# Sums of h finished ahead of the K/V block, key copies in fewer transfers, first compressed probabilities turned inside the attention slots

## The chip, the core and the metric

The kernel runs on one core of one Trainium2 chip. The metric is the device time of one execution in microseconds (us), lower is better. TensorE is called PE here (PEld its weight loads), VectorE DVE, ScalarE ACT, GpSimd POOL, SyncE SP. POOL and SP also issue the transfers (DMA).

## What is computed

One layer of a decoder trunk for 512 tokens of 2048 channels, all in float32. Of the reference, cut to what matters here:

```python
h = rms_norm(x, norm_g)
q, kv, g_logits, z_a, uv, z_b, merge_logits = split(h @ w_in)
k_c, v_c, k_s, v_s, k_w, v_w = split(kv, 6)        # 4 groups x 64 each
kc, vc = compress(k_c, ...), compress(v_c, ...)    # 32 -> 1 token, stride 16
# per head: softmax over compressed, selected and window keys, ALiBi slopes
o = g0 * softmax(q kc) vc + g1 * softmax(q k_s) v_s + g2 * softmax(q k_w) v_w
o_a = o * silu(z_a)
o_b = spatial_gating(uv) * silu(z_b)
merged = g_a * (o_a @ w_up_a) + g_b * (o_b @ w_up_b)
x = x + merged @ w_out
x = x + sigmoid(x @ w_ple_gate) * (p @ w_ple)
out = rms_norm(x, final_g)
```

## The kernel before

**Precision.** PE multiplies in a rounded float32 format, so each operand is split into a high part (a cast on ACT, `high`, line 158) and a low part (source minus high on DVE, `low`, line 164), and each product is three matmuls: high by high, high by low, low by high (lines 420 to 422, 446 to 448 and 459 to 461). The weights are streamed by SP into `raw` (three buffers) and split into `hi` and `lo`, or `hs` and `ls` in the blocks; `split_to` does it two steps ahead of the matmuls. `hi` has four buffers and `lo` three.

**One stream of matmuls.** All projections are jobs of one generator, `gemm`. `fill(n)` draws n units from it (a unit is three matmuls of 512 columns, about), `finish(name)` runs it to the end of a job. Between units the program places other work by hand. Three small queues hang on it: `deferred` (done at the next step's `flush`), `background` (taken at `state["pops"]` entries for each step) and `slow` (transfers that add up weights in DRAM for later blocks, taken at `state["rate"]` for each step; each is led by a one-column copy on ACT and POOL, `pad_r`, lines 378 and 379). Job order at the start: p by its weights (pl0 to pl3), kc0, vcg (compressed values and gate logits), kc1, q0, q1, kv, za0, q2, and so on.

**The K/V block** (`kv`) computes the selected and window keys and values, 1024 columns, with seven products in place of eight on 2x2 halves: products "1" to "7", four steps each, 12 matmuls of 512 columns a step (lines 420 to 422). The steps go in the order of `products(job)`: 1 and 5 in turn, 6 and 3 in turn, 7, then 2 and 4 in turn. Products 5, 6, 3 and 7 need sums of parts of h in place of h. The sums of weights are DVE subtractions (line 301).

**The sums of h** are made by `h_chunk(c)`, four chunks of four background entries: `whole`, `s1`, `s23`, `s4`. A chunk is eight additions or subtractions of 128x512 on DVE (line 504, into the scratch `o32`) and four splits (ACT cast, DVE low): into `ob_h` (sum 5), `ob_l` (sum 6), `vt` (sum 3) and into a pair of stream buffers of `hi` and `lo` (sum 7, tiles `h_hi` and `h_lo`). Each is then stored to DRAM by POOL (`hsum` line 528, `h3_d` line 535) for later blocks, and sum 7 is read back into `ob_h` before product 7 (line 828). The background begins with four splits of the compression weights `w1` (into `w1h` and a `b11` buffer).

**Keys.** When rows of keys are done, `turn_k(b, hf)` turns them on PE (`ps_kt`, line 592) and splits them into `ob_h` and `ob_l` (lines 597 and 603); b is 0 or 1 for the two branches. Each half (hf) is then copied to the other 64 partitions with four transfers by POOL (line 608), 16 in all.

**Between the block and the attention slots** six single units with flushes follow, then the first group's compressed attention is started: `cmp_scores` (two matmuls, line 1463, with `kcp`, that POOL clears at line 1325 and fills at line 1454), `cmp_softmax`, `cmp_weigh` (POOL multiplications, lines 1504 and 1505), `cmp_transpose` (line 1511), with 1, 3, 3, 5 and 1 units between. Then 48 slots of the attention follow (`slots`; a slot is a head pair ft, a block of 128 queries and one or both branches), with the units of the remaining q and za jobs spread over them. For groups 1 to 3, softmax, weighing and turning stand in the slots j = 1, 2 and 4 of ft = 2, 4, 6.

Some names share a tag in the profile: `o` is `o32`, `b` is a `b11` buffer (a q head pair after line 160 and 166), `c` is `c21`, `keep` the kept partial results of a block, `t` the DRAM sums of w_up_b.

Of the kernel before, what the change touches and what calls it, by code (L numbers as in the profile page):

```python
# [13 lines left out]
F32 = mybir.dt.float32  # L14
# [46 lines left out]
def products(job):  # L61

    if isinstance(job.order[0], tuple):
# [7 lines left out]
                             ("6", "0123"), ("7", "3"), ("5", "0123"), ("4", "1"), ("3", "0123")) for j in map(int, js)]  # L71
LATE_BANK = {"1": 0, "7": 0, "6": 1, "5": 1, "3": 1, "2": 2, "4": 3}


@with_exitstack
def kernel(ctx: ExitStack, tc: tile.TileContext, x, p, norm_g, w_in,
# [121 lines left out]
    def add_job(job):  # L198
        jobs.append(job)
        if job.kind == "S":  # L200
# [10 lines left out]
            if job.reload:  # L211
                for tags in (("b11", "b12"), ("b22",), ("b11'",), ("b21",)):
                    for j in range(half // 2):
                        for tag in tags:
                            c, k = (job.c0, c2)[tag[2] == "2"], half * (tag[1] == "2") + 2 * j
                            ld[tag, j] = add_load("b12" if tag == "b12" else "raw", weights(job, k, 2, c), 2, job.cols)
                for p, j in products(job):
                    for tag in {"5": ("b11",), "3": ("b22",), "7": ("b11'",), "4": ("b21", "b12")}.get(p, ()):
                        last_sub[ld[tag, j]] = len(subs)
                    subs.append((job, p, j, ld))  # L220
                return
# [287 lines left out]
    def parts_later(hi, lo, src, then=None):  # L509
# [9 lines left out]
        deferred.append(first)  # L519

    def h_chunk(c, temps, homes):

# [3 lines left out]
        def put(p, src):  # L526
            o = homes[p][:, k1]
            parts_later(o[:, :, lo_t], o[:, :, hi_t], src, lambda: nc.gpsimd.dma_start(hsum_dram[p][:, k1], o))

# [58 lines left out]
    def turn_k(b, hf):  # L588
# [10 lines left out]
        def lows():  # L599
            for a in range(2):  # L600
                for e in range(2):
                    g = kk(b, 2 * a + e)
                    nc.vector.tensor_tensor(out=ob_l[rows[e], g, sl], in0=ps[rows[e], a * 256:a * 256 + 256],
                                            in1=ob_h[rows[e], g, sl].bitcast(F32), op=ALU.subtract)
            for o in (ob_h, ob_l):
                for e in range(2):
                    g = slice(kk(b, e), 8, 4)
                    nc.gpsimd.dma_start(o[rows[1 - e], g, sl], o[rows[e], g, sl])
        deferred.append(lows)

    vc_rows = {}
# [210 lines left out]
    def evac_kv(p, ps):  # L822
# [3 lines left out]
        if p == "5":  # L826
            for c in range(4):
# [4 lines left out]
    add_job(Job("kv", "S", w_in, C_KV + 1024, 512, KT, lambda p, k, t: kv_act(p, k, t), evac_kv, ("s", "g", "t"),  # L832
                c2=C_KV + 512, reload=True))
    for s in "z0 q2 q3 z1 q4 q5 z2 q6 q7 z3 z4 z5 z6 z7".split():
# [368 lines left out]
    with tc.tile_pool(name="cmp", bufs=1) as cmp:  # L1203
# [24 lines left out]
        for c in range(4):  # L1228
            background.extend(h_chunk(c, lambda: [o32[:, i].rearrange("p (a t) -> p a t", a=2) for i in range(4)],
                                      {"5": ob_h, "6": ob_l, "3": vt_flat}))  # L1230
        state["pops"] = 0.75
        finish("kc0")
        state["pops"] = 0.4
        finish("vcg")
        state["pops"] = 0.75
        fill(4)
# [71 lines left out]
    assert not background  # L1308
    for _ in range(6):
        fill(1)  # L1310
        flush()
# [13 lines left out]
    nc.gpsimd.memset(kcp.bitcast(F32), 0.0)  # L1325
    nc.gpsimd.memset(vcb.bitcast(F32).rearrange("p i e -> p (i e)"), 0.0)
    b0 = att.tile([P, S], F32, name="b0")
# [192 lines left out]
    def cmp_values(ft):  # L1520
        b = bank("s", "ps_c")
        for n, i in enumerate((0, 1 + ft % 2)):
# [9 lines left out]
                            base=384, channel_multiplier=1)  # L1532
    cmp_scores(0, 0)
    for f, u in zip((partial(cmp_scores, a=1), cmp_softmax, cmp_weigh, cmp_transpose), (1, 3, 3, 5)):
        fill(u)
        flush()
        f(0)
    fill(1)
    n = len(slots)
# [6 lines left out]
    for s in range(n + 3):  # L1546
# [21 lines left out]
        if s < n:  # L1568
            if ft % 2 == 1 and ft < 7 and j == 3:
                events.append((cmp_keys, (ft + 1) // 2))  # L1570
            if ft % 2 == 0 and ft > 0 and j in (1, 2, 4):
                events.append(({1: cmp_softmax, 2: cmp_weigh, 4: cmp_transpose}[j], ft // 2))
            if ft % 2 and j == 3:
                events.append((cmp_values, ft))
# [612 lines left out]
```

## Time and profile before

| what | us |
|---|---|
| median of 3 runs | 1530.21 (1528.96 to 1530.72) |
| the profiled execution, device time | 1529.65 |
| its span, first to last instruction | 1527.9 |
| mean granted PE clock in it | 0.995 of full speed |

Times in the lines of the profile are us from the span's start; outside the span lie 1.75 us. A line of a group or of the timeline reads: line, engine, operation, out<-in, shape, count, and in brackets the idle time of the engine just before and what ended it. A table of windows gives an engine's busy time in each stretch (number of instructions in brackets), the granted PE clock, and how busy the 16 DMA engines were.

### The profile page before, as it was taken

How to read it: one execution, taken by the hardware profiler on the slowest of the kernel's cores; microseconds unless marked ns; L12 is line 12 of the kernel's file. 1: busy time of each engine (PE TensorE's matmuls, PEld its weight loads, DVE VectorE, ACT ScalarE, POOL GpSimd, SP SyncE). 2: the span in 40 equal slices, each digit the busy share in tenths (PEclk: the TensorE clock that was granted, in tenths of full speed). 3: DMA queues.
4: the chain of work that ended last, by engine and by line, in shares of the span. 5: the costliest groups of instructions: out<-in, count | busy, mean ns of one | idle time of the engine just before them, and what ended most of it. 6: DMA issues, size and time to landing. Idle time of an engine off the chain costs nothing.

```text
span 1527.9 us, 20459 instructions
## 1 busy us (share of the span) xinstructions
PE 1500.1 (98%) x7149; PEld 1252.8 (82%) x7149; DVE 1245.7 (82%) x1889; ACT 868.7 (57%) x1498; POOL 396.3 (26%) x617
## 2 busy tenths in 40 slices
PE   9998979999999999999999999999999999999997
PEld 8986868888888888888888888888888888888886
DVE  7598768998997788978897979797877985678877
ACT  6545446777775555545555565555446465544556
POOL 1222062334343232343334333431010002100000
PEclk9999999999999999999999999999999999999999
DMA  8577698889884985878586977896697769945555
GB/s 324 159 226 231 190 198 213 184 176 237 183 222 141 307 274 164 272 184 271 141 260 179 253 204 233 246 333 251 236 333 253 237 198 322 316 171 179 184 204 191
DMA packets 184855, 346.82 MB, mean 227 GB/s; under 512 B 15144, under 2 KB 77232, under 8 KB 181552
## 3 DMA queue, kind: packets, MB, share of 16 engines
q0 software_dynamic: 71696, 172.62, 41.4%
q1 hardware_dynamic: 112912, 172.64, 34.6%
q8 instruction: 56, 0.92, 0.2%
q14 instruction: 47, 0.39, 0.1%
q10 hardware_dynamic: 144, 0.26, 0.0%
HBM read 283.08 MB, written 109.58 MB: 257 GB/s over the span
## 4 chain that ended last, share of the span: by engine, by line
PE 90%; DVE 5%; issue 2%; ACT 1%; POOL 1%; DVEq 0%; POOLq 0%; ACTq 0%
PE ps_m L420 7%; PE ps_m L422 7%; PE ps_m L421 7%; PE ps_wo L421 3%; PE ps_wo L420 3%; PE ps_wo L422 3%; PE ps_t L1409 2%; PE ps_u L420 2%; PE ps_u L422 2%; PE ps_ub L421 2%; PE ps_ub L420 2%; PE ps_pg L422 2%; PE ps_pg L421 2%; PE ps_ua L421 2%; PE ps_ua L420 2%
## 5 line engine op out<-in xcount | busy, mean ns | idle before, releaser
L164 DVE TENSOR_TENSOR ls<-b,hs 128x1024 fp32r<-128x1024 f32 x224 | 273.7, 1222 | 112.2 <-ACT hs L158 110.8
L158 ACT CAST hs<-b 128x1024 fp32r<-128x1024 f32 x224 | 235.6, 1053 | 206.0 <-PE ps_m L422 47.5
L158 ACT CAST hs<-raw 128x1024 fp32r<-128x1024 f32 x130 | 136.9, 1054 | 126.7 <-issue 35.7
L164 DVE TENSOR_TENSOR ls<-raw,hs 128x1024 fp32r<-128x1024 f32 x130 | 158.7, 1221 | 40.1 <-ACT hs L158 39.8
L420 PE MATMUL ps_m<-hs,act_h 128*128 128x512 f32 x256 | 100.1, 391 | 0.0
L421 PE MATMUL ps_m<-ls,act_h 128*128 128x512 f32 x256 | 99.7, 389 | 0.0
L422 PE MATMUL ps_m<-hs,act_l 128*128 128x512 f32 x256 | 99.6, 389 | 0.0
L301 DVE TENSOR_TENSOR b<-raw,b 128x1024 f32<-128x1024 f32 x76 | 92.6, 1218 | 4.7 <-DMA raw<-in_w_in_dram 4.6
L164 DVE TENSOR_TENSOR lo<-raw,hi 128x512 fp32r<-128x512 f32 (+1 forms) x120 | 79.4, 666 | 19.7 <-issue 6.6
L158 ACT CAST hi<-raw 128x512 fp32r<-128x512 f32 (+1 forms) x120 | 70.4, 597 | 38.2 <-PE ps_vcg L461 11.5
L301 DVE TENSOR_TENSOR b<-b,b 128x1024 f32<-128x1024 f32 x72 | 87.6, 1217 | 0.0
L379 POOL COPY pad_r<-pad_r 128x1 f32<-128x1 f32 x40 | 34.9, 872 | 159.2 <-ACT pad_r L378 159.2
L158 ACT CAST pth<-ps_t 128x512 fp32r<-128x512 f32 (+1 forms) x88 | 47.7, 544 | 46.8 <-PE ps_t L1409 46.2
L1368 ACT ACTIVATE prob<-prob,st 128x512 f32<-128x512 f32 (+3 forms) x128 | 70.7, 556 | 4.8 <-DVE st L1359 4.7
L164 DVE TENSOR_TENSOR ptl<-ps_t,pth 128x512 fp32r<-128x512 f32 (+1 forms) x88 | 55.5, 636 | 11.8 <-ACT pth L158 11.1
L1359 DVE CUSTOM_DVE_ANT_0 prob<-ps_s,b 128x512 f32<-128x512 f32 (+3 forms) x128 | 56.1, 485 | 1.6 <-PE ps_s L1350 1.1
L422 PEld LDWEIGHTS ps_m<-hs,act_l 128*128 128x128 f32 x256 | 48.1, 188 | 10.1
L421 PEld LDWEIGHTS ps_m<-ls,act_h 128*128 128x128 f32 x256 | 48.1, 188 | 9.9
L420 PEld LDWEIGHTS ps_m<-hs,act_h 128*128 128x128 f32 x256 | 48.1, 188 | 9.8
L446 PE MATMUL ps_za<-act_h,hi 128*128 128x512 f32 x128 | 54.5, 426 | 0.0
L1384 DVE TENSOR_SCALAR prob<-prob,st,gates 128x512 f32<-128x512 f32 (+3 forms) x128 | 51.5, 454 | 1.8
L446 PE MATMUL ps_q<-act_h,hi 128*128 128x512 f32 x128 | 52.3, 409 | 0.0
(746 smaller groups left out, 4556.9 us busy)
## 6 DMA issues: line engine op xcount, KB each, us to landing
raw<-in_w_in_dram SPq DMA_DIRECT2D x112, 512.0 KB, 5.1
b<-in_w_in_dram SPq DMA_DIRECT2D x58, 512.0 KB, 6.6
o<-in_w_out_dram POOLq DMA_DIRECT2D x48, 512.0 KB, 7.9
t<-in_w_up_b_dram POOLq DMA_DIRECT2D x24, 512.0 KB, 8.5
raw<-in_w_ple_gate_dram SPq DMA_DIRECT2D x24, 512.0 KB, 3.8
b<-o SPq DMA_DIRECT2D x18, 512.0 KB, 6.5
o<-o POOLq DMA_DIRECT2D x16, 512.0 KB, 5.1
act_l<-gate POOLq DMA_DIRECT2D x8, 1024.0 KB, 13.2
```

Of the source, the lines that this page charges most:

```text
L158: nc.scalar.copy(hi, src)
L164: nc.vector.tensor_tensor(out=lo, in0=src, in1=hi.bitcast(F32), op=ALU.subtract)
L301: nc.vector.tensor_tensor(out=b[o], in0=b[x], in1=b[y], op=ALU.subtract)
L379: nc.gpsimd.tensor_copy(steps[:, 16 + i:17 + i], steps[:, i:i + 1])
L420: nc.tensor.matmul(o, ah, wh, start=st, stop=False, skip_group_check=go)
L421: nc.tensor.matmul(o, ah, wl, start=False, stop=False, skip_group_check=go)
L422: nc.tensor.matmul(o, al, wh, start=False, stop=sp, skip_group_check=go)
L446: nc.tensor.matmul(ps, hi[:, j], ah, start=st, stop=False)
L1359: nc.vector.tensor_tensor_reduce(out=pt[:, j * n:j * n + n], in0=o[:, j], in1=b0[:, 512 - n:], scale=-SLOPE[h], scalar=3.0e38, op0=ALU.add ...
L1368: nc.scalar.activation(sl, sl, AF.Exp, bias=st[:, 0, j, hh:hh + 1], scale=-1.0, accum_out=st[:, 1, j, hh:hh + 1])
L1384: nc.vector.tensor_scalar(out=sl, in0=sl, scalar1=st[:, 1, j, hh:hh + 1], scalar2=gates[:, i, gate:gate + 1], op0=ALU.mult, op1=ALU.mult)
L1409: nc.tensor.transpose(b[:, (2 * e + hh) * P:(2 * e + hh + 1) * P], pts[hh][:, c:c + P], ident)
```

## The change

- `h_chunk`: only the store of sum 5 is issued as soon as the sum is made. The stores of sums 6 and 3 are collected and put into the background behind the last chunk; there the rate falls to one entry for two steps. Ahead of it the rates are higher: 1, 0.8 and 0.7 entries a step (0.75, 0.4 and 0.75 before).
- The loads of the K/V block: the first b11 and b12, then b12 ahead of b11.
- The block's last steps go 2, 2, 4, 2, 4, 2, 4, 4 in place of 2, 4, 2, 4, 2, 4, 2, 4.
- Keys: the copies to the other partitions move both halves at once, four transfers for each b. Those of b = 0 follow its last low parts; those of b = 1 are issued behind `kcp`, the bias `b0` and the clearing of `vcb`.
- Behind the block the slow queue is stopped (rate 0), and 2, 2 and 1 units are drawn in place of six single ones.
- For the first group, `cmp_scores` and `cmp_softmax` come behind 3, 1 and 4 units, then 6 units; `cmp_weigh` and `cmp_transpose` move into slots 2 and 4 of ft = 0.

```diff
+PAIRS = [(p, j) for pair in ("15", "63") for j in range(4) for p in pair] + [("7", j) for j in range(4)] + [
+    ("2", 0), ("2", 1), ("4", 0), ("2", 2), ("4", 1), ("2", 3), ("4", 2), ("4", 3)]
...
-                for tags in (("b11", "b12"), ("b22",), ("b11'",), ("b21",)):
-                    for j in range(half // 2):
-                        for tag in tags:
...
+                first = [("b11", 0), ("b12", 0)] + [(t, j) for j in range(1, half // 2) for t in ("b12", "b11")]
+                for tag, j in first + [(t, j) for t in ("b22", "b11'", "b21") for j in range(half // 2)]:
...
+    stores = {"6": [], "3": []}
...
-            parts_later(o[:, :, lo_t], o[:, :, hi_t], src, lambda: nc.gpsimd.dma_start(hsum_dram[p][:, k1], o))
+            def store():
+                nc.gpsimd.dma_start(hsum_dram[p][:, k1], o)
+            parts_later(o[:, :, lo_t], o[:, :, hi_t], src, store if p == "5" else None)
+            if p != "5":
+                stores[p].append(store)
...
-            for o in (ob_h, ob_l):
-                for e in range(2):
-                    g = slice(kk(b, e), 8, 4)
-                    nc.gpsimd.dma_start(o[rows[1 - e], g, sl], o[rows[e], g, sl])
+            if not b and not hf:
+                deferred.append(partial(twin_keys, 0))
         deferred.append(lows)
+    def twin_keys(b):
+        halves = slice(0, 64), slice(64, 128)
+        for o in (ob_h, ob_l):
+            for e in range(2):
+                g = slice(kk(b, e), 8, 4)
+                nc.gpsimd.dma_start(o[halves[1 - e], g], o[halves[e], g])
...
-                c2=C_KV + 512, reload=True))
+                c2=C_KV + 512, order=PAIRS, reload=True))
...
-        state["pops"] = 0.75
+        background.append(lambda: [state.update(pops=0.5), background.extend(
+            stores["3"] + 2 * [lambda: None] + stores["6"])])
+        state["pops"] = 1
         finish("kc0")
-        state["pops"] = 0.4
+        state["pops"] = 0.8
         finish("vcg")
-        state["pops"] = 0.75
+        state["pops"] = 0.7
...
-    for _ in range(6):
-        fill(1)
+    state["rate"] = 0
+    for u in (2, 2, 1):
+        fill(u)
         flush()
...
-    nc.gpsimd.memset(vcb.bitcast(F32).rearrange("p i e -> p (i e)"), 0.0)
...
-    cmp_scores(0, 0)
-    for f, u in zip((partial(cmp_scores, a=1), cmp_softmax, cmp_weigh, cmp_transpose), (1, 3, 3, 5)):
+    nc.gpsimd.memset(vcb.bitcast(F32).rearrange("p i e -> p (i e)"), 0.0)
+    twin_keys(1)
+    for f, u in zip((partial(cmp_scores, a=0), partial(cmp_scores, a=1), cmp_softmax), (3, 1, 4)):
         fill(u)
         flush()
         f(0)
-    fill(1)
+    fill(6)
...
-            if ft % 2 == 0 and ft > 0 and j in (1, 2, 4):
+            if ft % 2 == 0 and (ft > 0 and j == 1 or j in (2, 4)):
                 events.append(({1: cmp_softmax, 2: cmp_weigh, 4: cmp_transpose}[j], ft // 2))
```

What it does to the engines' queues is shown at three places. A row is line, operation, out<-in and shape; x2 are two in a row. The lines of the changed file are numbered on from the old ones: 164 is 168 there, 301 is 304, 504 is 507, 166 is 170, 1325 is 1343, 1454 is 1471, 1177 is 1192, 608 is 624.

First, DVE's queue in the second half of the job vcg, before: the low parts of vcg's weights (128x304), the last w1 split and the first additions of chunk 0.

```order
L164 TENSOR_TENSOR lo<-raw,hi 128x304 x2
L164 TENSOR_TENSOR b_596<-o_582,b_594 128x8x64
L164 TENSOR_TENSOR lo<-raw,hi 128x304 x3
L504 TENSOR_TENSOR o_582<-act_h_88,act_l_89 128x512 x2
L164 TENSOR_TENSOR lo<-raw,hi 128x304
L164 TENSOR_TENSOR lo<-raw,hi 128x512
L504 TENSOR_TENSOR o_582<-o_582,act_h_92 128x512
L504 TENSOR_TENSOR o_582<-o_582,act_l_93 128x512
```

The same stretch now, up to the last low part of vcg's weights and the first of kc1's (128x512):

```order
L168 TENSOR_TENSOR lo<-raw,hi 128x304
L507 TENSOR_TENSOR o_582<-act_h_92,o_582 128x512
L507 TENSOR_TENSOR o_582<-o_582,act_l_93 128x512
L168 TENSOR_TENSOR ob_l<-o_582,ob_l 128x2x256
L168 TENSOR_TENSOR h_lo<-o_582,h_hi 128x512
L168 TENSOR_TENSOR lo<-raw,hi 128x304
L168 TENSOR_TENSOR vt<-o_582,vt 128x2x256
L168 TENSOR_TENSOR lo<-raw,hi 128x304
L507 TENSOR_TENSOR o_582<-act_h_88,act_l_89 128x512 x2
L168 TENSOR_TENSOR lo<-raw,hi 128x304
L507 TENSOR_TENSOR o_582<-o_582,act_h_92 128x512
L507 TENSOR_TENSOR o_582<-o_582,act_l_93 128x512
```

Two whole chunks now stand where half of one stood: between any two low parts of weights there are two to four instructions of the sums.

Second, DVE's queue where the K/V block begins, before: from the first sum of weights (b12x) to the second (b12y). `b_1325<-ps_q_1213` is the low part of q1, which frees q1's bank for the block.

```order
L301 TENSOR_TENSOR b12x<-b12x,raw 128x1024
L164 TENSOR_TENSOR ls<-raw,hs 128x1024
L504 TENSOR_TENSOR o_582<-o_582,act_h_94 128x512
L504 TENSOR_TENSOR o_582<-o_582,act_l_95 128x512
L164 TENSOR_TENSOR ls<-b12x,hs 128x1024
L504 TENSOR_TENSOR o_582<-o_582 128x512 x2
L164 TENSOR_TENSOR ob_h<-o_582,ob_h 128x2x256
L164 TENSOR_TENSOR ob_l<-o_582,ob_l 128x2x256
L164 TENSOR_TENSOR h_lo<-o_582,h_hi 128x512
L166 SCALAR_TENSOR_TENSOR b_1325<-ps_q_1213,b_1325 64x512 x2
L301 TENSOR_TENSOR b12y<-b12y,raw 128x1024
```

The same stretch now:

```order
L304 TENSOR_TENSOR b12x<-b12x,raw 128x1024
L168 TENSOR_TENSOR ls<-raw,hs 128x1024
L507 TENSOR_TENSOR o_582<-act_h_94,o_582 128x512
L507 TENSOR_TENSOR o_582<-o_582,act_l_95 128x512
L168 TENSOR_TENSOR ls<-b12x,hs 128x1024
L168 TENSOR_TENSOR vt<-o_582,vt 128x2x256
L170 SCALAR_TENSOR_TENSOR b_1350<-ps_q_1239,b_1350 64x512 x2
L304 TENSOR_TENSOR b12y<-b12y,raw 128x1024
```

Three instructions of the sums (the end of chunk 3) stand between in place of seven, and behind them none follow, where before 15 more came among the block's own.

Third, POOL's queue from the last copies of keys to `kcp`, before:

```order
L608 DMA ob_h<-ob_h 64x2x256 x2
L608 DMA ob_l<-ob_l 64x2x256 x2
L379 COPY pad_r<-pad_r 128x1
L1177 DMA t_105<-in_w_up_b_dram 128x2x512
L1325 MEMSET kcp 128x160
L1326 MEMSET vcb 128x384
L1454 CAST kcp<-o_582 128x32 x2
```

Now, from `kcp` on; the copies of b = 0 stand ahead of the first row:

```order
L382 COPY pad_r<-pad_r 128x1
L1192 DMA t_105<-in_w_up_b_dram 128x2x512
L1343 MEMSET kcp 128x160
L1471 CAST kcp<-o_582 128x32 x2
L1547 IOTA b_2010 128x512
L1548 AFFINE_SELECT b_2010<-b_2010 128x512
L1550 MEMSET vcb 128x384
L624 DMA ob_h<-ob_h 64x2x512 x2
L624 DMA ob_l<-ob_l 64x2x512 x2
```

The last copies of keys, which wait for the last low parts, have moved behind `kcp`.

More of the change, by code (lines that the diff above doesn't have):

```diff
@@ L211, in add_job @@
             if job.reload:
-                for tags in (("b11", "b12"), ("b22",), ("b11'",), ("b21",)):
-                    for j in range(half // 2):
-                        for tag in tags:
-                            c, k = (job.c0, c2)[tag[2] == "2"], half * (tag[1] == "2") + 2 * j
-                            ld[tag, j] = add_load("b12" if tag == "b12" else "raw", weights(job, k, 2, c), 2, job.cols)
+                first = [("b11", 0), ("b12", 0)] + [(t, j) for j in range(1, half // 2) for t in ("b12", "b11")]
+                for tag, j in first + [(t, j) for t in ("b22", "b11'", "b21") for j in range(half // 2)]:
+                    c, k = (job.c0, c2)[tag[2] == "2"], half * (tag[1] == "2") + 2 * j
+                    ld[tag, j] = add_load("b12" if tag == "b12" else "raw", weights(job, k, 2, c), 2, job.cols)
                 for p, j in products(job):
```

## The prediction

> **What bounds the kernel now.** The page first: which engine is full.
>
> ```profile
> span 1527.9 us, 20459 instructions
> PE 1500.1 (98%) x7149; PEld 1252.8 (82%) x7149; DVE 1245.7 (82%) x1889; ACT 868.7 (57%) x1498; POOL 396.3 (26%) x617
> ```
>
> PE is idle for 27.8 us in all. The change leaves PE's instructions as they are, only in another order; so it can win no more than idle time, and time in which PE runs at a lower clock. Second, PE's waits: whom did it wait for?
>
> ```profile
> PE ps_c L1463 <- POOL kcp L1454: 5.9, 1, 5.9
> PE ps_kv L420 <- DVE b L166: 3.9, 1, 3.9
> ...
> PE ps_c L1511 <- POOL b L1505: 1.7, 1, 1.7
> ...
> PE ps_q L448 <- DVE lo L164: 1.3, 1, 1.3
> ```
>
> All four (total, times, longest) lie between 93 and 228 us, where the change works; nothing later waits over half a microsecond in all. Third, the windows around the two long waits, cut at 3.41 us, with PE's busy time, number of instructions, granted clock.
>
> ```profile
> 116.43:119.84 3.41, 1.79 (x8) 1.00 0.96 350
> 119.84:123.25 3.41, 1.12 (x5) 1.00 0.73 270
> 123.25:126.66 3.41, 3.41 (x10) 0.50 0.95 244
> 126.66:150.00 23.34, 21.20 (x88) 1.00 0.57 178
> ...
> 212.00:215.41 3.41, 1.95 (x5) 0.50 1.20 239
> 215.41:218.83 3.42, 3.42 (x10) 0.50 0.52 92
> ```
>
> A wait is paid twice: after it PE runs at half clock, 3.41 us after the first, and from 212.0 to 218.83 after the second. In the 23 us behind the first, PE is idle for another 2.1.
>
> **Term 1: ahead of the block and at its start.** What holds PE at the block's start is seen in DVE's timeline (start, duration, instruction).
>
> ```profile
> 110.86 1.21 DVE L301 TENSOR_TENSOR b12x<-b12x,raw 128x1024 f32<-128x1024 f32 x1
> 111.99 1.22 DVE L164 TENSOR_TENSOR ls<-raw,hs 128x1024 fp32r<-128x1024 f32 x1
> 113.13 0.68 DVE L504 TENSOR_TENSOR o<-o,act_h 128x512 f32<-128x512 f32 x1
> 113.84 0.69 DVE L504 TENSOR_TENSOR o<-o,act_l 128x512 f32<-128x512 f32 x1
> 116.17 1.23 DVE L164 TENSOR_TENSOR ls<-b12x,hs 128x1024 fp32r<-128x1024 f32 x1 [1.64 <-ACT hs L158]
> 117.32 1.41 DVE L504 TENSOR_TENSOR o<-o 128x512 f32<-128x512 f32 x2
> 118.65 0.68 DVE L164 TENSOR_TENSOR ob_h<-o,ob_h 128x512 fp32r<-128x512 f32 x1
> 119.25 0.68 DVE L164 TENSOR_TENSOR ob_l<-o,ob_l 128x512 fp32r<-128x512 f32 x1
> 119.85 0.68 DVE L164 TENSOR_TENSOR h_lo<-o,h_hi 128x512 fp32r<-128x512 f32 x1
> 120.59 1.39 DVE L166 SCALAR_TENSOR_TENSOR b<-ps_q,b 64x512 fp32r<-64x512 f32 x2
> ```
>
> PE waits until 122.13 for the last row, q1's low part, which stands behind seven instructions of the sums. Each takes DVE 0.60 (rows 118.65 to 119.85, start to start) to 0.71 (113.13 to 113.84); I take 0.65. The change puts 19 of the sums' 48 instructions ahead of b12x that stood behind it: 19 x 0.65 = 12.4 us. Is there room? DVE's busy time in the stretches ahead:
>
> ```profile
> 53.19:74.00 20.81, 11.57 (x22) 1.00 0.63 170
> 74.00:92.90 18.90, 16.00 (x38) 1.00 0.63 183
> 92.90:110.86 17.96, 15.80 (x33) 1.00 0.86 268
> ```
>
> Up to 92.9, 12.1 us are idle. There stands the low part that PE waits for already (1.3, above), and by the queues the 19 instructions all stand ahead of it now: 33 of the sums, before 14. The sums cannot start ahead of the w1 splits, so I hold some 10.4 of the 12.1 us reachable. DVE comes 12.4 - 10.4 = 2.0 us late, and PE with it. The bounds: all hidden, and the 1.3 us gained as well; or half of the room reachable, 12.4 - 6 = 6.4 us late.
>
> From there to b12x the queue holds 12 instructions of the sums, before and now: DVE keeps its 2.0 us, and some of a microsecond is lost where it waits for ACT; b12x at about 113.5. From b12x to the end of q1's low part took 122.0 - 110.9 = 11.1; now four instructions of the seven are gone, 2.6 less, 8.5: it ends at 122.0. PE itself, 2.0 late, wants it at about 120, waits 2.0 in place of 4.1, and goes on at 122.0, where it did before. **Term 1: -0.1**; from -3.5 (DVE not late) to +4.3.
>
> **Term 2: the half clock at 123.25** cost half of 3.41 us. The window ahead of it held 1.12 us of matmuls, 33% of 3.41; the one before held 1.79, 52%, and did not bring it. A wait of 2.0 us leaves 41% if one window holds all of it, which 1.41 in 3.41 positions do; then it is as likely as not. I take it as gone, 4 in 5. **Term 2: -1.7**, or 0.
>
> The Trainium skill (TensorE: Matmul & The Clock Gate, Part 1: The HAM clock gate) has the clock halved after at least one idle window of about 3.4 us, counted by a free-running counter. The free-running window agrees with the two starts, 88.75 us or 26 windows apart; an idle one does not: the row with 1.12 us of work was enough. By the page no wait of 2.0 us could bring the half clock, and term 2 would be sure.
>
> **Term 3: the rest of the block.** The 2.1 us idle in 126.66 to 150 go with the 15 instructions of the sums that stood among the block's low parts; I leave 0.3 for ACT, which there copies kept results between its casts. **Term 3: -1.8**, from -2.1 to -1.0. The stores of sums 3 and 6 now come two steps apart, behind no one who waits: POOL has nothing else there that PE needs, and the DMA engines were 0.57 busy. The loads come in another order by the same three `raw` buffers; the b21 slots are held two steps longer, and a load takes little of the five steps between its issue and its use:
>
> ```profile
> raw<-in_w_in_dram SPq DMA_DIRECT2D x112, 512.0 KB, 5.1
> ```
>
> Against 5.1 us stand five steps of 12 matmuls at 0.24 (21.20 us for 88, above), 14.4 us. If that cover went, a step would wait some 3 us.
>
> **Term 4: the compressed keys.** POOL's timeline, then PE's:
>
> ```profile
> 204.76 1.21 POOL L608 DMA_DIRECT2D ob_h<-ob_h  x2 [4.39 <-ACT ob_h L597]
> 206.47 1.18 POOL L608 DMA_DIRECT2D ob_l<-ob_l  x2 [0.50 <-DVE ob_l L603]
> 207.64 1.18 POOL L608 DMA_DIRECT2D ob_h<-ob_h  x2
> 208.81 1.18 POOL L608 DMA_DIRECT2D ob_l<-ob_l  x2
> ...
> 211.32 1.18 POOL L1177 DMA_DIRECT2D t<-in_w_up_b_dram  x1 [1.14 <-DMA ob_h<-ob_h]
> ...
> 212.81 0.60 POOL L1454 CAST kcp<-o 128x32 fp32r<-128x32 f32 x2
> ```
>
> ```profile
> 202.74 0.48 PE L446 MATMUL ps_za<-act_h,hi 128*128 128x512 f32 x1
> ...
> 207.17 0.39 PE L448 MATMUL ps_za<-act_h,lo 128*128 128x512 f32 x1
> 213.46 1.22 PE L1463 MATMUL ps_c<-b,kcp 128*128 128x512 f32 x2 [5.91 <-POOL kcp L1454]
> ```
>
> POOL issues eight copies, 0.6 each, and one transfer, ahead of `kcp`. Now only the copies of b = 0 stand there, four, whose last low parts are ready inside the block:
>
> ```profile
> 195.35 1.75 DVE L603 TENSOR_TENSOR ob_l<-ps_kt,ob_h 64x256 fp32r<-64x256 f32 x4
> ```
>
> From 197.1 four issues take 2.4 us, or 4.8 if one of double size takes double; the transfer and the copy ahead of it 1.4; the clearing and the casts 1.3. `kcp` is ready by 202 to 205, at the earliest when the block's buffers are free (203). PE asks for it after eight units of three matmuls, 0.72 each, behind 202.7, at 208.5 by the clock of before: over 3 us of cover. The wait of 5.9 goes, and with it the half clock over PE's 5.37 us from 213.46 to 218.83, 2.7. **Term 4: -8.6.** Next late would be the copies of b = 1: POOL stands at them until DVE's last low parts (near 209), then issues 2.4 to 4.8 us; they must land before the second slot, 11 more units on and a slot further. A copy landed in at most
>
> ```profile
> DMA to landing us min/median/max: 4.0/4.9/6.3
> ```
>
> 6.3 us (tile `ob_h`, 190 to 240 us): by 220 at the latest; PE is there at 202.7 + 19 x 0.72 = 216.4 plus some 2 of compressed scores and 4 of the first slot, 222. If it lacked, PE would wait that difference.
>
> **Term 5: weighing.** PE's 1.7 us for L1505 go: the turning now stands two slots behind POOL's multiplications. The other three groups do so already, and the row counts one wait, not four. **Term 5: -1.7.** Costed at nothing: the order of the block's last steps and fewer slow transfers by one ahead of the slots (a later one takes its place; none is awaited near).
>
> **The sum** against the execution profiled: 1529.65 - 0.1 - 1.7 - 1.8 - 8.6 - 1.7 = 1515.75. The median of the runs is 0.6 above that execution: 1516, rounded down a little.
>
> **The rivals.**
> 1. *DVE is later than 2.0 us.* For it: from 86 to 94 DVE is busy without a gap, and with three `lo` buffers it cannot run ahead far. Term 1 at its upper bound, and half clock in the new wait: 1516 + 4.4 + 1.7 = 1522. Against it: 9.2 us idle in vcg alone. Chance 0.16.
> 2. *`kcp` stays late.* It lies in memory that the block gives back, so its clearing may wait for the last reader, and POOL may come to it behind a transfer that waits for a landing, as the 1.14 above. If half of the wait stays, 3 us, with its half clock of 2.7: 1516 + 5.7 = 1521.7. Against it: 3 us of cover. Chance 0.12.
> 3. *Slower: the weights' buffers wait for the stores of sum 7.* `h_hi` and `h_lo` take turns in the `hi` and `lo` buffers, and a part keeps its buffer until its store has landed:
>
> ```profile
> L460 PE MATMUL ps_vcg<-lo,act_h x64: 296/301/409, 47.2 to 74.0; 128*128 128x304 f32 x64
> ...
> L535 POOL DMA_DIRECT2D h_d<-h_lo x4: 721/724/731, 84.9 to 144.5; - x4
> ...
> DMA to landing us min/median/max: 3.4/5.3/8.0
> ```
>
> The part keeps its buffer from its low part (0.7) over POOL's two issues (2 x 0.72) to the landing, 5.3 to 8.0: 7.4 to 10.1 us. Now two chunks fall into vcg, whose 16 steps of four such matmuls take 26.8 / 16 = 1.68 each; three `lo` buffers come round in 5.0, so the weights wait 2.4 to 5.1 us for each chunk. In kc1 and q0 a round takes three steps of 12 x 0.24, 8.6, and the wait is 0 to 1.5. At the upper ends, 2 x 5.1 + 2 x 1.5 = 13.2, and behind each of the two long ones half clock as behind the wait of 5.9, 2.7 each: 1516 + 13.2 + 5.4 = 1534.6, slower than now. It decides where landings reach the longest of the four, 8.0, and PE has no step in hand; for it: four chunks now go through in about the time of two. Against it: at the median landing it costs 2 x 2.4 = 4.8 and half of these are DVE's own idle time; no wait of PE above names such a buffer. Chance 0.04.
>
> **How the numbers follow.** A measurement of this kernel can tell some 0.2%, 3.1 us, from no change. The forecast, every term within its bounds and none of the rivals, 1516, has 0.62; the three rivals 0.16, 0.12 and 0.04; 0.06 remains for waits that I have not seen, a third of that beyond 1533.3. The forecast runs from 1511.5, with term 1 at its lower bound and the last idle microsecond gone (-3.5 + 0.1 - 0.3 - 0.8), to 1518.5, with term 2 at nothing and term 3 at -1.0. Rivals 1 and 2 end at 1522 and need some room above, as their prices are half of a wait: the range is 1511 to 1524. Faster: the forecast, rivals 1 and 2 and a third of the rest, 0.92, less 0.04 for rivals 1 and 2 together (1516 + 6.1 + 5.7 = 1527.8): 0.88. Same: that 0.04 and a third of the rest, 0.06. Slower: rival 3 and the last third, 0.06.
>
> **What would show it.** In PE's waits: no row for `kcp` and none for L1505's successor; the wait of the block's first matmul for a `b` tile at 2.0 or less; the wait for a low part in q0 (1.3) at about 3.3, since DVE's 2.0 us arise there. In windows of 3.41 us: no granted clock of 0.50 between 110 and 225. In DVE's windows: 53 to 74 nearly full, over 18 of 20.81. PE's idle time between the block's first step and 150 at 0.3. Wrong it would be if PE waits for `lo` over 5 us between 47 and 103 (rivals 1 and 3: in the first it names DVE at the first steps of q0, in the third already in vcg), if `ps_c` waits for `kcp` or for a landing (rival 2), or if a new wait for loads stands where steps of products 2 and 4 were exchanged.

## The result, and the profile after

The changed kernel takes 1519.38 us (median of 4 runs, 1517.54 to 1520.95) against 1529.59 for the one before in the same rounds: ratio 0.9933, interval 0.9915 to 0.995. It is faster by 10.2 us; 13.9 were forecast. The profiled execution is the longest of the four, 1520.95, 8.7 below the one profiled before. Two executions in the experiments' rounds, 2153.25 us of sums_only and 2154.04 of the kernel before, ran at a granted clock of 0.654 throughout and are left out of every median and range. The page and PE's waits (who waited for whom; total, times, longest):

```profile
span 1519.2 us, 20444 instructions
...
PE 1498.4 (99%) x7149; PEld 1251.9 (82%) x7149; DVE 1244.9 (82%) x1889; ACT 869.4 (57%) x1498; POOL 392.7 (26%) x609
```

```profile
PE ps_q L451 <- DVE lo L168: 2.5, 1, 2.5
PE ps_m L424 <- DVE ls L168: 1.4, 1, 1.4
PE ps_vct L638 <- ACT o L630: 1.4, 1, 1.4
...
PE ps_kv L423 <- DVE b L170: 1.4, 1, 1.4
...
PE ps_vct L638 <- issue: 0.4, 1, 0.4
```

The waits for `kcp` (5.9), for POOL's multiplication (1.7) and for the block's own low parts (1.8) are gone, and that at the block's start fell from 3.9 to 1.4. Three are new or larger: `ps_vct`, the turning of vcg's values while kc1 runs (0.4 and 1.4); the low part in q0 (1.3 before); and one in `ps_m`, the products of w_up, where the change touches nothing. PE's windows (busy, instructions, granted clock, share of the DMA engines), around the wait in q0 and at the block's start:

```profile
96.29:99.70 3.41, 0.93 (x6) 1.00 1.07 296
99.70:103.11 3.41, 3.41 (x15) 0.50 0.38 110
103.11:106.53 3.42, 3.42 (x24) 1.00 0.96 353
...
123.25:126.66 3.41, 2.01 (x9) 1.00 1.04 378
126.66:150.00 23.34, 23.34 (x103) 1.00 0.74 226
```

The half clock that stood at the block's start now follows the wait in q0. From 126.66 to 150 PE is never idle (2.1 us before).

For all twelve experiments the rest is read from one table: four stretches, cut at the first or last matmul of vcg, the block, the first slot, za and the products of w_up, from the profiled executions, in us. What is left out differs by at most 0.9 ahead of the first stretch and 0.9 in all behind it. Some of these executions lie well off their kernel's median: keys_slots 3.6 above it, calm 2.3, keys_first 2.0, old_steps 3.9 below.

| kernel | vcg's start to block's end | to first slot | to the end of za | w_up's products |
|---|---|---|---|---|
| before | 154.0 | 27.6 | 262.6 | 313.5 |
| changed | 153.2 | 16.1 | 264.2 | 315.7 |
| sums_only | 151.6 | 26.7 | 263.0 | 313.8 |
| keys_only | 154.0 | 19.7 | 264.9 | 316.5 |
| keys_slots | 154.0 | 16.6 | 271.2 | 315.4 |
| own_hi | 151.2 | 16.1 | 263.7 | 315.7 |
| slow_back | 153.2 | 16.1 | 266.7 | 313.6 |
| sums_pause | 156.5 | 16.1 | 265.6 | 315.5 |
| keys_first | 151.7 | 17.5 | 266.1 | 317.1 |
| weigh_early | 151.6 | 19.2 | 264.8 | 315.6 |
| old_steps | 151.6 | 16.6 | 266.0 | 315.3 |
| whole_pool | 154.2 | 16.2 | 265.9 | 315.8 |
| calm | 152.7 | 16.2 | 264.8 | 313.6 |
| both | 155.5 | 16.1 | 263.6 | 313.5 |

The gain of the changed kernel is 0.8 up to the block's end and 11.5 behind it; 1.6 is given back among the slots and 2.2 some 800 us later.

The changed kernel was not run again beside the experiments, so that "slower than the changed kernel" below compares medians of different rounds. The kernel before took 1528.75 to 1530.13 in the experiments' rounds. The ratios are each against the kernel before in the same rounds; where an interval overlaps 0.9915 to 0.995, that of the changed kernel, the difference is not clear of the noise.

### The profile page after: what moved, and what is told of

It is laid out like the page before. It is cut to its first block, busy times and chain, and to the rows that moved or that the text cites. A ratio compares the mean times of both kernels' runs of the same rounds, so it can differ in the third digit from the quotient of the medians.

```text
span 1519.2 us, 20444 instructions
## 1 busy us (share of the span) xinstructions
PE 1498.4 (99%) x7149; PEld 1251.9 (82%) x7149; DVE 1244.9 (82%) x1889; ACT 869.4 (57%) x1498; POOL 392.7 (26%) x609
## 4 chain that ended last, share of the span: by engine, by line
PE 86%; DVE 6%; DMA 4%; issue 2%; ACT 1%; POOL 1%; DVEq 0%; ACTq 0%; POOLq 0%
PE ps_m L424 5%; PE ps_m L425 5%; PE ps_m L423 5%; PE ps_wo L424 3%; PE ps_wo L425 3%; PE ps_wo L423 3%; DMA ob_d<-pt_g 2%; PE ps_u L425 2%; PE ps_ub L425 2%; PE ps_ub L423 2%; PE ps_pg L424 2%; PE ps_pg L423 2%; PE ps_ua L425 2%; PE ps_ua L423 2%; PE ps_zb L425 2%
## 5 line engine op out<-in xcount | busy, mean ns | idle before, releaser
L424 PEld LDWEIGHTS ps_m<-ls,act_h 128*128 128x128 f32 x256 | 48.1, 188 | 11.7 <-DVE ls L168 1.9
L451 PE MATMUL ps_q<-act_h,lo 128*128 128x512 f32 x128 | 50.6, 395 | 2.5 <-DVE lo L168 2.5
```

The lines of the kernel that those rows point to most:

```text
L424: nc.tensor.matmul(o, ah, wl, start=False, stop=False, skip_group_check=go)
L451: nc.tensor.matmul(ps, lo[:, j], ah, start=False, stop=sp)
```

## The experiments

### The parts alone: keys_slots, sums_only, keys_only

Edits: `keys_slots` has the hunks from `twin_keys` on (keys, stopped slow queue, weighing and turning in the slots); `sums_only` the others (`h_chunk`, rates, loads, steps of the block). `keys_only` against `keys_slots`:

```diff
-    for f, u in zip((partial(cmp_scores, a=0), partial(cmp_scores, a=1), cmp_softmax), (3, 1, 4)):
+    for f, u in zip((partial(cmp_scores, a=0), partial(cmp_scores, a=1), cmp_softmax, cmp_weigh, cmp_transpose), (3, 1, 3, 3, 4)):
...
-    fill(6)
...
-            if ft % 2 == 0 and (ft > 0 and j == 1 or j in (2, 4)):
+            if ft % 2 == 0 and ft > 0 and j in (1, 2, 4):
```

Expected of keys_slots:

> The kernel before with the parts on the keys and on the first group's weighing and turning; the sums of h, the loads and the order of the block's steps stay as before. Prediction's terms 4 and 5: 1529.6 - 8.6 - 1.7 = 1519.3. Theory H (the sums ahead give back what they win, since a store of sum 7 holds a buffer of the weights and makes ACT, then DVE late): as fast as the changed kernel within 2 us, 1518 to 1520, with the waits at 92, 122 and 138 to 149 us as before and the half clock behind the one at 122, but no wait for kcp and none for L1505. Rival R (the sums ahead are worth the 3.6 us that the prediction gave, and the changed kernel lost its time later, in the products of w_up): 3 us or more slower than the changed kernel, 1522 to 1523.

Expected of sums_only:

> The kernel before with the sums of h ahead, the delayed stores, the order of loads and of the block's steps; keys and compressed attention as before. Theory H: 0 to 2 us faster than before, 1528 to 1530, with ACT waiting some 3.5 us for the landing of h_hi near 69, PE 1.8 us for ps_vct and 2.5 for q0's low part, the half clock behind that, and the 5.9 us for kcp untouched. Rival R: 3.6 faster, 1526.

Expected of keys_only:

> The kernel before with the keys' part alone; weighing and turning of the first group stay ahead of the slots (3 and 4 units apart). Both theories: term 4 alone, 8.6 faster than before, 1521.0, and the wait of PE for L1505 stays at 1.7 to 2.4 (the turning has 4 units in place of 5 ahead of it). If the wait of 1.7 and a second one only moved with kcp, no row for L1505 is left and it is as fast as the kernel with both parts.

Measured: keys_slots 1525.33 us (1519.94 to 1532.95), ratio 0.9971 (0.9957 to 0.9986); sums_only 1527.97 (1526.31 to 1529.70), 0.9987 (0.9978 to 0.9996); keys_only 1526.12 (1524.49 to 1527.28), 0.9974 (0.9965 to 0.9984). The sums' part took the time that theory H gave, at its fast end; the keys' part did not: keys_slots was to take 1518 to 1523 and keys_only 1521.0 by either theory. The two parts give 4.7 and 2.0 us alone and 10.2 together: no theory had that. In the table the keys' part does what it should, 7.9 less up to the first slot, and weighing in the slots 3.1 more, but among the slots keys_slots loses 8.6 in the execution profiled, 1528.91. Who waits there, in keys_slots from 200 to 260 us:

```profile
ACT hi L158 <- DMA raw<-in_w_in_dram: 7.6, 1, 7.6
...
PE ps_t L1414 <- DVE ptl L164: 5.8, 1, 5.8
```

and its transfers from 195 to 240 us (KB of one, median us to landing), ahead of the same rows of the changed kernel and of the row of the weights in the kernel before:

```profile
t<-in_w_up_b_dram POOLq DMA_DIRECT2D x13, 512.0 KB, 12.3
raw<-in_w_in_dram SPq DMA_DIRECT2D x6, 512.0 KB, 16.9
```

```profile
t<-in_w_up_b_dram POOLq DMA_DIRECT2D x13, 512.0 KB, 10.2
raw<-in_w_in_dram SPq DMA_DIRECT2D x6, 512.0 KB, 10.0
```

```profile
raw<-in_w_in_dram SPq DMA_DIRECT2D x6, 512.0 KB, 9.5
```

A weight load took 5.1 us over the whole kernel before and 9.5 in this stretch of it; here it takes 16.9, beside 13 slow transfers as before. One came so late that ACT stood 7.6 us at its cast; the high parts of the probabilities stood behind that cast in ACT's queue, DVE's low parts behind those, and PE waited 5.8, with half clock from 235.42 to 242.25, where PE has 4.25 us of work: 5.8 + 2.1 of the 8.6. Why the loads are late here and not in the changed kernel, the two rows do not say.

### A buffer for sum 7: own_hi

```diff
-            o = [stream.tile([P, 2, 256], F32R, tag=tag, name="h_" + tag, bufs=n) for tag, n in (("hi", 4), ("lo", 3))]
+            o = [stream.tile([P, 2, 256], F32R, tag=tag, name="h_" + tag, bufs=n) for tag, n in (("hi", 4), ("lo", 3))[c < 3:]]
+            if c < 3:
+                o.insert(0, o32[:, 7].rearrange("p (a t) -> p a t", a=2).bitcast(F32R))
```

The reason for it, in ACT's timeline of the changed kernel (start, duration, instruction, in brackets the idle time before and what ended it):

```profile
72.19 0.45 ACT L162 CAST hi<-raw 128x304 fp32r<-128x304 f32 x1 [3.47 <-DMA h_d<-h_hi]
...
77.04 0.62 ACT L162 CAST vt<-o 128x512 fp32r<-128x512 f32 x1 [1.22 <-DVE o L507]
...
78.20 0.37 ACT L630 COPY o<-ps_vcg 128x256 f32<-128x256 f32 x1
```

ACT waits 3.47 us until sum 7's store has landed: that is rival 3's mechanism. The copy of vcg's result, which PE waits for, starts at 78.20; before, at 74.34.

> The changed kernel, but the high part of sum 7 of chunks 0 to 2 goes into a free row of the scratch o32 in place of a buffer of the weights. Theory H: ACT's wait of 3.5 us near 69 goes, the eviction of vcg starts some 3.5 us earlier (near 74.7), PE's wait for ps_vct (1.8) goes, the low part that q0 waits for comes up to 3.5 earlier, so that the 2.5 us and the half clock behind it (1.6) go as well: 4 to 6 us faster than the changed kernel, 1513 to 1515. Rival N (it is the number of the sums' instructions on DVE, 19 more ahead of q0's low part): ps_vct no longer waits, but the low part comes at most 1 us earlier and the half clock stays: 1517 to 1519.

Measured: 1520.10 us (1517.75 to 1521.01), ratio 0.9931 (0.9919 to 0.9943): as the changed kernel. ACT's timeline in it:

```profile
71.03 0.62 ACT L162 CAST ob_h<-o 128x512 fp32r<-128x512 f32 x1 [2.90 <-DVE o L507]
...
76.43 0.62 ACT L162 CAST vt<-o 128x512 fp32r<-128x512 f32 x1 [1.30 <-DVE o L507]
...
77.60 0.37 ACT L632 COPY o<-ps_vcg 128x256 f32<-128x256 f32 x1
```

ACT's wait for the landing is gone, and ACT waits for DVE's sums in its place; the copy comes only 0.6 earlier, PE's 1.4 for it and 2.4 in q0 stay. Theory H falls as it was put, with ACT's wait as the cause. But the edit moves only the high part of sum 7; the low part still holds a `lo` buffer. DVE's timeline of the changed kernel, then of own_hi:

```profile
72.67 0.48 DVE L168 TENSOR_TENSOR lo<-raw,hi 128x304 fp32r<-128x304 f32 x1 [1.07 <-ACT hi L162]
```

```profile
72.06 0.48 DVE L168 TENSOR_TENSOR lo<-raw,hi 128x304 fp32r<-128x304 f32 x1 [1.07 <-DMA h_d<-h_lo]
```

DVE stands as long as before, now for the landing of the low part's store, and its queue is 0.6 ahead already at 53 us. So the stores' 1.07 us of DVE are still in own_hi, and no run takes them out. Around them DVE has no idle time of over 0.5 us from 58 to 78 us, which speaks for the sums' work on DVE as the larger part (rival N). Of N's own signs only the late low part is there: `ps_vct` still waits, and no half clock is left.

The first stretch is 2.0 shorter than in the changed kernel all the same, but it is 1.5 or 1.6 shorter in four kernels with the sums unchanged too (sums_only, keys_first, weigh_early, old_steps: 151.6 or 151.7). The windows of sums_only around the wait for `ps_vct` show what differs:

```profile
78.60:82.01 3.41, 1.70 (x7) 1.00 0.77 187
82.01:85.42 3.41, 3.41 (x12) 0.50 0.77 203
85.42:88.84 3.42, 3.42 (x17) 1.00 0.55 153
```

There half clock follows the wait for `ps_vct`, in kc1; DVE catches up while PE is slow, q0's wait is 1.2 in place of 2.5, and no half clock follows it. The other three show the same, with half clock from 81 or 82 us on. In slow_back and calm, which also have the changed kernel's instructions up to the block's end, it comes at 99 us as in the changed kernel, and the stretch takes 153.2 and 152.7. In own_hi the wait of 2.4 in q0 brought none at all, for it lies across the edge of two windows:

```profile
93.13:96.54 3.41, 2.46 (x11) 1.00 0.93 172
96.54:99.95 3.41, 1.99 (x13) 1.00 0.80 215
```

So the same instructions end the block up to 1.6 us apart, as the windows happen to lie. The changed kernel's four runs, 1517.54, 1518.26, 1520.50 and 1520.95, lie in two pairs some 2.8 apart. That the pairs have this cause is argued: only one of the four was profiled, and 1.6 is not 2.8.

### Fewer sums around the evictions: sums_pause

```diff
-        state["pops"] = 0.7
+        state["pops"] = 0.3
...
+        state["pops"] = 1
         quad["b12"].append(partial(ring, 2, F32))
```

> The changed kernel with fewer sums around the evictions of vcg and kc1: 0.3 background entries a step from kc1 to the compression's products, 1 behind them (0.7 throughout before). Some six sums less stand ahead of the low part that q0 waits for; four more stand behind b12x. Theory C (a chain across two in-order queues: ACT's casts of the sums wait for DVE's sums, the evictions of kc1 stand behind those casts on ACT, and the low part stands behind the evictions on DVE): the 2.5 us in q0 and the half clock behind it go, the wait at the block's start (1.4) grows to 1.5 to 3: 1 to 3 us faster than the changed kernel. Rival D (DVE's work up to the block's start is one sum, and where it stands does not matter): what q0 no longer waits comes back at the block's start, with its half clock; within 1 us of the changed kernel.

Measured: 1525.09 us (1521.88 to 1529.65), ratio 0.9974 (0.9965 to 0.9984), 5.7 slower than the changed kernel. PE's waits:

```profile
PE ps_kv L423 <- DVE b L170: 3.9, 1, 3.9
...
PE ps_q L451 <- DVE lo L168: 0.5, 1, 0.5
```

What q0 no longer waits (2.5 to 0.5) came back at the block's start (1.4 to 3.9), as rival D says. The time is worse than it said, 156.5 up to the block's end: the clock is at half from 80.28 to 83.70, behind `ps_vct`, and again from 124.66 to 131.48, three windows where the changed kernel has one.

### The sums' first additions on POOL: whole_pool

```diff
-                add(w[n], act_h(k1, t), act_l(k1, t))
+                nc.gpsimd.tensor_tensor(out=w[n], in0=act_h(k1, t).bitcast(F32), in1=act_l(k1, t).bitcast(F32), op=ALU.add)
```

> The changed kernel with the first two additions of each chunk of sums (whole, eight in all) on POOL in place of DVE: some 5.2 us less of DVE ahead of the block. Theory D (DVE's work up to the block's start is one sum, and PE waits for what does not fit): the waits of PE for ps_vct (1.8), in q0 (1.2 to 2.5) and at the block's start (1.4), with one half clock (1.6), shrink by 3 to 5 us together: 1514.5 to 1516.5. Rival Q (POOL's queue holds the additions behind its stores, which wait for DVE's low parts, so that DVE then waits for POOL): DVE shows waits for POOL of 1 us or more in each chunk, and the time is the same or longer, 1519 to 1522.

Measured: 1524.51 us (1524.10 to 1526.09), ratio 0.9968 (0.9957 to 0.998), 5.1 slower than the changed kernel. Neither theory: DVE does not wait for POOL's results. DVE's timeline, then POOL's:

```profile
67.11 0.47 DVE L168 TENSOR_TENSOR lo<-raw,hi 128x304 fp32r<-128x304 f32 x1
...
68.27 2.84 DVE L168 TENSOR_TENSOR lo<-raw,hi 128x304 fp32r<-128x304 f32 x1
```

```profile
68.23 2.54 POOL L551 TENSOR_TENSOR o<-act_h,act_l 128x512 f32<-128x512 f32 x2
```

A low part of this form took 0.47 us, and 2.84 while POOL's two additions ran: it ended 0.3 behind them. Two more low parts, beside the additions of other chunks, took 3.37 and 3.58 us, where this form (128x512) takes 0.68. DVE's busy time from 53 to 122 us rose from 58.6 in the changed kernel to 61.8, though eight additions less stand there. The Trainium skill (SBUF — State Buffer, Who interferes with whom) says that a DVE instruction with two SBUF inputs contends with a GpSimd instruction that reads SBUF. The trace agrees. In PE's waits that is 1.5 us more in vcg (2.0) and 0.6 less in q0 (1.9), 1.0 up to the block's end; another 1.7 of the profiled execution is lost among the slots, where the weights' loads take 15.5 us to landing (195 to 240 us); why they do is not shown.

### The slow queue: slow_back and calm

```diff
-    state.update(rate=1.3, step=None, due=0, late=0.6)
+    state.update(rate=1.3, step=None, due=0, late=1.6)
```

The wait in `ps_m`: POOL's timeline of the changed kernel, then ACT's and PE's:

```profile
987.21 0.64 POOL L382 COPY pad_r<-pad_r 128x1 f32<-128x1 f32 x1 [4.62 <-ACT pad_r L381]
987.79 1.15 POOL L1192 DMA_DIRECT2D o<-in_w_out_dram  x1
988.50 1.70 POOL L1896 DMA_DIRECT2D ob_l<-oa_d  x2
```

```profile
1012.31 0.62 ACT L162 CAST pt_g<-ob_f 128x512 fp32r<-128x512 f32 x1 [5.04 <-DMA ob_d<-pt_g]
```

```profile
1015.98 0.50 PE L424 MATMUL ps_m<-ls,act_h 128*128 128x512 f32 x1 [1.44 <-DVE ls L168]
```

Before, the last slow transfer went out at 987.7 and the loads of `ob_l` apart, at 993.4 and 999.9:

```profile
987.72 1.15 POOL L1177 DMA_DIRECT2D o<-in_w_out_dram  x1
...
993.44 0.58 POOL L1878 DMA_DIRECT2D ob_l<-oa_d  x1
999.92 0.55 POOL L1878 DMA_DIRECT2D ob_l<-oa_d  x1 [5.90 <-PE ps_m L422]
```

Now one more stands ahead of these (the one before it was issued at 977.4), and when it has gone, at 988.5, both go at once. The stores of `pt_g` land after 10.2 us there (median; 7.0 in the same stretch before), ACT waits 5.0 for one, and PE in the end.

> The changed kernel with one number changed: the slow queue, which is stopped behind the block, does one more transfer as it starts again (late 1.6 in place of 0.6), so that from there on it stands where it stood before. Theory S (the stopped queue is one transfer behind for the rest of the program; that transfer, an in_w_out load, goes ahead of the 1 MB loads of ob_l near 988 us, the landings there grow to 13 us, and PE waits 1.4 us near 1016): that wait goes, 2 to 2.5 us faster than the changed kernel. Rival: the wait near 1016 comes from something else that the keys' part moved; no change within 0.7 us.

Measured: 1521.94 us (1520.18 to 1524.17), ratio 0.9952 (0.994 to 0.9963): not faster, against the 2 to 2.5 us that theory S gave. But the wait near 1016 is gone, and w_up's products take 313.6 in place of 315.7. The time went elsewhere, in PE's waits:

```profile
PE ps_t L1426 <- DVE ptl L168: 3.0, 2, 2.8
```

The transfer that was put back now goes out at the first slots, where the weights' loads now take 18.7 us to landing (195 to 240 us; 10.0 in the changed kernel), and 2.5 us are lost there. So the other way to catch up:

```diff
-    state.update(rate=1.3, step=None, due=0, late=0.6)
+    state.update(rate=0.9, step=None, due=0, late=0.6)
...
-        if s == 43:
-            state["rate"] = 0
+        if s in (8, 43):
+            state["rate"] = 1.45 if s == 8 else 0
```

> The changed kernel with another rate of the slow queue: 0.9 transfers a step in the first eight slots and 1.45 from there to slot 43 (1.3 before), so that it stands where it stood before from slot 43 on. Theory S with theory B (at the first slots the DMA engines are the bound, 13 slow transfers from 195 to 240 us hold up the loads of the weights): no wait near 1016, and no new one in the slots, where the kernel with late 1.6 got 2.8 us: 2 to 3.5 us faster than the changed kernel, 1516 to 1517.5, and from the first slot to the end of za 262.5 to 264 us. Rival: the higher rate later makes loads late there, as much as is won.

Measured: 1517.26 us (1516.11 to 1519.57), ratio 0.9916 (0.9903 to 0.993), 2.1 less than the changed kernel by the medians and the fastest of all, though the intervals overlap. 313.6 in w_up's products, no long wait in the slots. Theory S holds: in all five kernels whose slow queue is not behind there (before, sums_only, slow_back, calm, both) the products take 313.5 to 313.8, in all nine others 315.3 to 317.1. Theory B does not follow: from the first slot to the end of za calm takes 264.8, no less than the changed kernel, though in an execution 2.3 above calm's median.

`both` is calm with the additions on POOL.

> Both of these together. If theories D, S and B all hold: 1512 to 1514. If only the additions on POOL do harm (rival Q): 1517 to 1519, that is calm plus what whole_pool shows over the changed kernel.

Measured: 1521.19 us (1520.02 to 1523.02), ratio 0.9945 (0.9932 to 0.9957): 3.9 above calm, as whole_pool is 5.1 above the changed kernel; 155.5 up to the block's end.

### Order of the copies of keys: keys_first

```diff
+    twin_keys(1)
     nc.gpsimd.memset(kcp.bitcast(F32), 0.0)
...
-    twin_keys(1)
```

> The changed kernel, but the merged copies of the second half of the keys are issued ahead of kcp's clearing, as before, not behind. Theory O (the order made the gain, not the smaller number of transfers): they wait for DVE's last low parts near 206.5, kcp is ready near 211 in place of 203.4, and PE waits some 3 us for it, with half clock behind it: 4 to 6 us slower than the changed kernel. Rival M (the merging made it): kcp comes by 208 and PE waits under 1 us; no change within 1 us.

Measured: 1521.99 us (1518.78 to 1526.97), ratio 0.9954 (0.9937 to 0.9971). POOL's timeline, then PE's wait:

```profile
206.54 0.37 POOL L1472 CAST kcp<-o 128x32 fp32r<-128x32 f32 x2
```

```profile
PE ps_c L1481 <- POOL kcp L1472: 1.0, 1, 1.0
```

Between the two theories: counted from the block's end, `kcp` starts 11.7 us later before (201.1 to 212.8), 8.0 here (198.5 to 206.5) and 2.6 in the changed kernel (200.3 to 202.9). Four issues less and one slow transfer less bring 3.7 and the order 5.4; but PE asks at 7.2, so only 1.0 of the wait comes back, and 1.4 up to the first slot. The ratio's interval overlaps the changed kernel's.

### Weighing ahead of the slots: weigh_early

The changed kernel with keys_only's edit.

> The changed kernel, but weighing and turning of the first group stand ahead of the slots again, 3 and 4 units behind the softmax. Term 5 alone: PE waits 1.7 to 2.4 us for POOL's multiplication, 2 us slower than the changed kernel. Rival: the first slots then come that much later, and loads that are late there (a DMA share over 1 from 195 to 235) are less late, so that less than 1 us is lost.

Measured: 1522.83 us (1520.91 to 1525.73), ratio 0.996 (0.9948 to 0.9972). PE's wait:

```profile
PE ps_c L1528 <- POOL b L1522: 2.4, 1, 2.4
```

19.2 against 16.1 up to the first slot; some of the 3.1 is the turning's own matmuls, which the changed kernel has behind that mark. By the medians 3.5 are lost (the intervals just overlap): more than the wait, and more than forecast. Half clock follows the wait and costs half of PE's 3.21 us in this window, 1.6 more:

```profile
218.20:221.62 3.42, 3.21 (x8) 0.50 1.11 240
```

### The old order of the block's last steps: old_steps

```diff
-                c2=C_KV + 512, order=PAIRS, reload=True))
+                c2=C_KV + 512, reload=True))
```

> The changed kernel with the block's last steps in the old order, 2, 4, 2, 4, 2, 4, 2, 4. Theory P (the new order is what lets the keys' part pay: the last keys are turned and kcp is cleared 2 us earlier, and the loads of the first q and za weights stand better against the transfers there, which the kernel with old sums and old order could not use, 1525): kcp is cleared near 205 in place of 202.6, loads come late in the slots, from the first slot to the end of za over 266 us in place of 264.2, 2 to 5 us slower than the changed kernel. Rival, as the prediction had it (the order costs and wins nothing): within 1 us of the changed kernel, 1518.5 to 1520.5.

Measured: 1524.93 us (1518.63 to 1529.74), ratio 0.9966 (0.9952 to 0.9979), 5.5 slower than the changed kernel by the medians. Weight loads from 195 to 240 us, then PE's wait:

```profile
raw<-in_w_in_dram SPq DMA_DIRECT2D x5, 512.0 KB, 17.7
```

```profile
PE ps_t L1426 <- DVE ptl L168: 1.9, 2, 1.7
```

17.7 us to landing against 10.0, as in keys_slots (16.9), and PE waits for a low part of the probabilities as there. The execution profiled (1521.05) loses 1.8 among the slots by it; most runs lost more, and none of those was profiled. That the order is worth some 5 us is measured by the medians, with the two intervals only just apart (0.995 and 0.9952) and the fastest of the ten runs as fast as the changed kernel. That it works through these loads is what the two profiles suggest; slow_back and whole_pool, with the new order, have loads as late (18.7 and 15.5), so that the old order is not the only thing that makes them late. How, whether by when a load's buffer comes free or by what it meets on the DMA engines, stays open.

## Why the prediction was right, and where its steps failed

The direction and the range held (1519.38 in 1511 to 1524). Against the execution of before, 13.9 were summed and 8.7 came, by these terms:

- **Term 4 and 5** (-8.6 and -1.7): the sum was right, -9.9 from the block's end to the end of za. `kcp` was ready at 203.4, within the 202 to 205 given. That merging, with one slow transfer less, would nearly have done it, keys_first shows by its wait (1.0). Of the two, 4 is smaller and 5 larger: with `kcp` early but the weighing in its old place PE waits 2.4, not 1.7, and half clock follows, so each hid some of the other.
- **Term 2 and 3** (-1.7 and -1.8): right in their places. No half clock at the block's start, a wait of 1.4 there, nothing idle from 126.66 to 150 (-2.1).
- **Term 1** (-0.1; profiled about +3, the -0.8 of the whole stretch less -2.1 and -1.7): mis-sized. PE was to go on at the block's start where it did before (122.13); it does at 126.60, 4.5 later, 1.7 of it by the half clock in q0. Some 1.5 comes back inside the block beyond terms 2 and 3, which no row here explains. The failing step is that "some 10.4 of the 12.1 us" of DVE's idle time were reachable. DVE's windows after:

```profile
53.19:74.00 20.81, 18.32 (x34) 1.00 0.73 192
74.00:92.90 18.90, 16.84 (x39) 1.00 0.58 164
```

  4.6 us are still idle, so 7.6 were reached, and 12.4 - 7.6 = 4.8 is how late DVE should come. It came 5.1 us late to q0's low part (98.77 against 93.65 by PE's start), not 2.0. In 2.9 of the 4.6 us DVE waits for ACT: 1.3 for the gates, behind a cast that waits for DVE's own sums, 1.1 for a cast that waits for a store of sum 7 to land, 0.5 for the first w1 split. PE paid while kc1 ran (0.3 and 1.8) and in q0 (2.5), where I had put it in q0 alone, with a half clock that only changed its place. That is between the forecast and rival 1 (+4.4 and 1.7). In the four kernels that end the block after 151.6 it is 1.6 less.
- **Rival 3** named the store of sum 7 that holds a weight's buffer. It is there: 3.47 us of ACT, and through it 1.1 of DVE. What these cost PE is open: own_hi, which frees the high part's buffer alone, shifts DVE's 1.1 us to the low part's store and is no faster.
- **"Costed at nothing"** failed twice. The slow queue, one transfer behind, was to be awaited nowhere near; it cost 2.2 us near 1016, 800 us on. The order of the block's last steps is worth some 5 us by the medians; I had looked only at whether its own loads had cover, not at what runs beside the loads behind it. Both are of one kind: the DMA engines were a resource that I had no term for. Their share (last but one column) from 195 to 235 us, before and after:

```profile
195.00:235.00 40.00, 31.76 (x134) 0.91 1.04 221
```

```profile
195.00:235.00 40.00, 39.57 (x195) 1.00 1.17 257
```

  The share was over 1 before, too; that PE's two long waits in this stretch had given the loads their time, and took it with them, is argued, not shown.

## What to carry to other kernels

A wait that is removed lets the next stage start earlier, into whatever transfers run there: look at the landing times of its loads in that stretch, and not at the share of the DMA engines alone, before the whole wait is booked as a gain. A queue that is drawn from at a rate has a memory: stop it for a few steps and the transfer that is left over turns up at its end; count where it stands at the later marks, and restore it where the engines have room. And moving work ahead on a full engine pays by the idle time that its queue can truly reach, with the other engine's casts and evictions in order between.

## What the runs showed of the hardware

- Half clock follows a window of 3.41 us that is partly busy: 0.93 us of work (27%) and 1.70 (50%) brought it, 1.79 (52%, before the change) and 2.01 (59%) did not. The edge is not sharp: 1.86 (55%) brought it in weigh_early. The Trainium skill (TensorE: Matmul & The Clock Gate, Part 1: The HAM clock gate) asks for an idle window; here half an idle one was enough. So a wait of 2.4 or 2.5 us costs 0 or 1.7 more by where the window's edge falls: none in own_hi, where the edge parts it, 1.7 in the changed kernel. This differs between executions of the same instructions.
- A DVE instruction with both inputs in SBUF took 2.84 us while POOL added, against 0.47.
- With a share of the DMA engines over 1 (195 to 240 us), a load of 512 KB took 6.5 (both) to 18.7 us (slow_back) to land by the medians, where 5.1 is the median of the whole kernel before. The share does not rank them: 10.0 at 1.16 in the changed kernel, 16.9 at 1.07 in keys_slots.
